# A hybrid trunk layer on one core: a list scheduler inside the kernel draws up every engine's order

## The chip, the core and the metric

The kernel runs on one core of a Trainium2 chip. The metric is device time in microseconds, the median of several runs. Three runs of the kernel before took 1523.97, 1532.54 and 1538.36 us, so the median is 1532.54 us.

## The reference

One residual layer over 16 learned meta tokens and 1024 tokens of width 1024, all float32:

- Input: RMS norm `hn` of the tokens, then one input projection `proj = hn @ w_in` to 7832 channels, split into three groups of heads.
- Gated DeltaNet, 6 heads of 128: causal convolution of four taps and SiLU on q, k, v; L2 norms of q and k; a gated delta rule over the tokens (`S_t = exp(g_t) (I - beta_t k_t k_t^T) S_{t-1} + beta_t k_t v_t^T`, `o_t = S_t^T q_t / sqrt(128)`); RMS norm and SiLU gate.
- RWKV-7, 8 heads of 64: token shift, low-rank decays and in-context rates, the recurrence `S_t = S_{t-1} diag(w_t) + (S_{t-1} a_t) b_t^T + v_t k_t^T`, group norm, a bonus term, SiLU gate.
- Mamba-2, 12 heads of 64 in 4 groups: convolution and SiLU, a chunked state-space scan, skip term, SiLU gate, grouped RMS norm.
- Output: `out = mixed @ w_out` (2048 to 1024), RMS norm, added to the input. The meta tokens are dropped.

## The kernel before, in words

Tokens lie along the free axis for the projections. The normalised input is kept in two float32r parts (`hh`, `hl`), each weight tile of 128 channels too, and a projection of one tile is three pieces of some 346 tokens, each of 8 x 3 matrix products that add up in one PSUM bank (`proj`, L154). In the profile these are the rows `pj`. The output projection works the same way on `ome`/`omw` and `ow` (rows `po`), with 512 columns a product.

The scans are cut into twelve units: six heads of DeltaNet (`unit_a`, a0 to a5), four pairs of heads of RWKV-7 (`unit_b`, b0 to b3) and two of Mamba-2 (`unit_c`, c0 and c1). Each unit first projects what its scan starts from ("proj"), then runs through small products in float32 with evacuations on ScalarE and VectorE between them ("scan"). Units a and b also solve triangular systems in blocks of 32 on VectorE (`solve32`, L189; rows `s_tmp`, `alb`, `blb`), after a trip through DRAM that regroups the blocks. Small products run on part of the array: 32 x 32 in the merges (`am`, `bm`), 64 rows or columns in `bsi`, `bu`, `bgr`. Values, queries and gates are projected later, when the scan needs them soon (`later`). Products of the units by name: `akT` starts the scan part of a unit a and `aoT` ends it; `bw` and `byT` do so for b, `cxT` and `cyT` for c. `unit_o` does the output projection in two halves: the first 512 columns with the channels that are finished, as a filler beside the last scans, and the rest when no other unit is active ("hold").

What sets the order: every unit is a generator that yields after a part. `schedule` (L1169 on) keeps a clock that adds up a rough length of what TensorE is given (`Meter`, L79), and an estimate of how long a scan part's results take to come back (`lag`). It emits the next scan part when its estimated time has come, and one product of a projection otherwise. Units start in the order of `PLAN`, when their tiles fit in the 26 slots of the pool. A unit's scan gets one of two lanes with two PSUM banks each; the lane with fewest units is taken, so units can share one. The framework then orders the emitted instructions on every engine by its own cost model and by priority: evacuations of projections are emitted with `high_priority(EVA)`, 700, scan parts with `PRI`, 300, and the solver's parts with `CALM`, 1500. It places all semaphores. SP issues the loads and stores.

Of the kernel before, what the change touches and what calls it, by code (L numbers as in the profile page):

```python
# [14 lines left out]
F32 = mybir.dt.float32  # L15
# [7 lines left out]
KT = 8  # L23
# [14 lines left out]
LOOK, LATE, EVAC, DMA = 0.05, 0.3, 2.0, 5.0  # L38
NOA = 3
PIPE = 0.5  # L40
HURRY, DUES = 60, (50, 60, 45, 55, 25, 60)
GATE = 9
XP = 500
# [6 lines left out]
SLOW = 1.0  # L50
# [28 lines left out]
class Meter:  # L79
    """An engine that adds up about how long what it is given takes: on the tensor engine, or on the way back to it."""  # L80

    def __init__(self, trunk, engine, fixed, each):
        self.trunk, self.engine, self.fixed, self.each = trunk, engine, fixed, each

    def __getattr__(self, name):
        op = getattr(self.engine, name)

        def call(out, *args, **kw):
            n = int(np.prod(out.shape[1:]))
            if name == "matmul":  # L90
                self.trunk.pe += n / 2400 if args[0].dtype == F32R else max(n, args[0].shape[-1]) / 600
            elif name == "transpose":
                self.trunk.pe += n / 1200
            elif not self.trunk.aside:
                self.trunk.lag += self.fixed + n * self.each
            return op(out, *args, **kw)  # L96

        return call


class Trunk:
    def __init__(self, tc, a):
        self.tc, self.nc, self.a = tc, tc.nc, a
        self.lane, self.pe, self.lag, self.aside = 0, 0.0, 0.0, False
        self.fetched, self.prefetch = {}, lambda i: None
        nc = tc.nc
        self.engines = tuple(Meter(self, e, f, n) for e, f, n in (
            (nc.vector, 0.25, 1 / 960), (nc.scalar, 0.3, 1 / 1200), (nc.tensor, 0, 0), (nc.gpsimd, 0.3, 1 / 500), (nc.sync, DMA, 0)))

    @contextmanager  # L110
    def off(self):
        """For instructions that nothing in their part waits for."""
        self.aside = True
        yield
        self.aside = False

# [11 lines left out]
    def tmp2(self, name):  # L128
        return self.sm.tile([128, 2, 128], F32, tag="t2", name=name, bufs=1)
# [12 lines left out]
    def weights(self, i):  # L142
        nc = self.nc
# [10 lines left out]
    def proj(self, i, pieces, evac, halo=0):  # L154
        """Channels of tile i, tokens along the free axis; a piece starts halo tokens early."""
        w = self.fetched.pop(i, None) or self.weights(i)
        for n, (a, b) in enumerate(pieces):
            a0 = max(a - halo, 0)
            p = self.pp.tile([128, 512], F32, tag="proj", name=f"pj{i}_{n}")
            for kt in range(KT):  # L160
                for m, (x, h) in enumerate(((0, self.hh), (0, self.hl), (1, self.hh))):
                    self.engines[2].matmul(p[:, : b - a0], w[kt // 4][:, x, kt % 4, :], h[:, kt, a0:b],
                                           start=(kt == 0 and m == 0), stop=(kt == KT - 1 and m == 2))
                    yield
            with self.tc.high_priority(EVA):
                evac(p, a, b, a - a0)
# [3 lines left out]
    def conv(self, i, cw, acc, bias=None, pieces=FULL):  # L170
        """Projection, causal convolution of four taps, halved (taps and bias hold halves), and silu(2x) = x tanh(x) + x."""
# [30 lines left out]
    def setup(self):  # L202
# [15 lines left out]
        pk = cp.tile([128, sum(n for _, n in PACK)], F32, tag="pack", name="pack")  # L218
# [23 lines left out]
        for cc in XG:  # L242
# [5 lines left out]
            with self.tc.high_priority(XP):  # L248
# [14 lines left out]
        # the gates are computed with tanh of the half; derived per-channel scalars of the RWKV group  # L263
# [7 lines left out]
    def scalars(self):  # L271
        """Per-token step sizes, decays and gates of the DeltaNet and Mamba groups."""
# [36 lines left out]
        # softplus(x) = max(x, 0) + log1p(u), u = exp(-|x|); log1p(u) = 2 atanh(u / (2 + u))  # L309
# [43 lines left out]
        # the same decays with tokens along the free axis, through DRAM, to be repeated over partitions  # L353
# [12 lines left out]
    def unit_a(self, h):  # L366
# [16 lines left out]
        # decays between the tokens of a chunk (rows the earlier one), masked before the exponential  # L383
# [12 lines left out]
        # |k|^2 and |q|^2 of each token  # L396
# [4 lines left out]
        for cc, p in transposed(k, "akT", groups):  # L401
# [6 lines left out]
            yield PIPE  # L408
        # the system is solved for the new values over bd = beta / |k|^2 and |k|
# [11 lines left out]
        # lo <- the strict part  # L421
        for gi, cc in enumerate(groups):
# [7 lines left out]
            yield PIPE  # L430

        # blocks of 32, solved with one block per partition
# [16 lines left out]
        yield 0.0  # L449
# [8 lines left out]
        # the values; up <- attention  # L458
        yield from self.wait(valued)
        vt = self.one([128, 9, 128], f"avt{h}")  # L460
        for cc, p in transposed(v_, "avT", groups):
# [3 lines left out]
            yield PIPE  # L465
        yield from self.wait(asked)
        for cc, p in transposed(q, "aqT", groups[:2]):
# [3 lines left out]
            yield PIPE  # L471
        v.tensor_scalar(ss[:, 9:], ss[:, 9:], EPS, None, ADD)
        self.rsqrt(rs[:, 9:], ss[:, 9:], "a_q")
        self.lag = 0.0
        for gi, cc in enumerate(groups[:2]):
# [6 lines left out]
            yield PIPE  # L482
        yield 7
        # dd: the blocks not transposed; merge 32 -> 64
# [10 lines left out]
        for i, (f, s) in enumerate(fs):  # L495
# [4 lines left out]
            yield 0.6  # L500
        for i, (f, s) in enumerate(fs):
# [4 lines left out]
            if i == 0:  # L506
                yield 0.6
# [4 lines left out]
                yield 0.3  # L512
        yield
        # merge 64 -> 128
# [20 lines left out]
        # the scan over chunks  # L535
        oss = sm.tile([128, 8], F32, tag="a_oss", name="a_oss", bufs=3)
        st = None
        for c in range(9):
# [22 lines left out]
            if c:  # L561
# [7 lines left out]
                self.lag = max(0.2, self.lag - 0.43)  # L569
# [3 lines left out]
        # rms norm of o (with q's norm and 1/sqrt(dk) folded in), gate  # L573
# [21 lines left out]
    def shifted(self, i, ti, t, gate=False):  # L595
        """Projection, mixed with the token before; PADB zero tokens in front. t: chunks of 64. gate: 2 silu of it."""
# [21 lines left out]
    def b_low(self):  # L618
        """The low-rank inputs of all heads, split in two, kept in DRAM."""
# [9 lines left out]
        # of both, the rounded part over its rest  # L629
# [8 lines left out]
    def unit_b(self, p):  # L638
# [11 lines left out]
        # each factor carries its decay to or from the chunk's end  # L650
# [12 lines left out]
        for i, (out, bias) in enumerate(((e1[:, :, 1:], self.w0), (at, self.a0))):  # L663
            for s, e in ((0, 8), (8, 16), (16, 17)):
# [4 lines left out]
                yield PIPE  # L669
# [499 lines left out]
    def schedule(self, plan, out, swap):  # L1169
# [29 lines left out]
        def step(s):  # L1199
            if s["want"] is not None:  # L1200
                s["has"], s["want"] = s["want"], None
# [173 lines left out]
```

## Time and profile before

| | |
|---|---|
| median of three runs | 1532.54 us |
| lowest and highest run | 1523.97 and 1538.36 us |
| span of the profiled execution, first to last instruction | 1518.0 us |
| mean granted TensorE clock | 0.970 |
| TensorE records (share of the span) | 1427.0 us (94%) |
| VectorE, ScalarE, GpSimd | 1014.6, 647.8, 239.2 us |
| instructions | 25,931, of which 9657 matrix products |

The profile is of one execution, and its span leaves out what lies before the first and after the last instruction; the views show no time for that. Matrix products are pipelined and their ends are modelled, so their records overlap: a covered TensorE is not one at its peak, and the pace is read from one start to the next. The granted clock (PEclk) is 1.00 at 2.4 GHz and 0.50 at 1.2 GHz. Names on the left of an arrow are written, those on the right read.

### The profile page before, as it was taken

The numbers are of one execution on the slowest core, as the hardware profiler recorded it, in microseconds if no ns is written. First come the engines' busy times: TensorE is split into PE (matmuls) and PEld (weight loads), VectorE is DVE, ScalarE is ACT, GpSimd is POOL, SyncE is SP. The second block draws the span as 40 slices with busy tenths as digits, with TensorE's granted clock in tenths as the row PEclk, the third lists the DMA queues.
The fourth block names the chain that finished last, engine by engine and source line by source line (L and its number), as shares of the span: only waits on it lengthen the run. The fifth ranks groups of instructions, "written<-read, shape, count | busy, mean of one in ns | idle before, by whom it ended". The sixth has DMA issues, their size and how long they took to land.

```text
span 1518.0 us, 25931 instructions
## 1 busy us (share of the span) xinstructions
PE 1427.0 (94%) x9657; PEld 1259.6 (83%) x9657; DVE 1014.6 (67%) x2688; ACT 647.8 (43%) x1814; POOL 239.2 (16%) x227
## 2 busy tenths in 40 slices
PE   4999999999999999997999999999999999889897
PEld 3988878887888888987888898899998988678686
DVE  7549695476659456869735699745489967542573
ACT  5354351334434352443635534433456154532530
POOL 2122011011101111223101221102232111200100
PEclk9999998899999999999989999989999999999999
DMA  5221211111011121211111111101322111552851
GB/s 187 58 85 43 70 33 39 29 41 64 29 30 47 49 74 43 86 31 53 46 43 50 43 46 53 36 29 57 97 59 61 43 36 44 169 159 89 250 193 56
DMA packets 102880, 104.28 MB, mean 69 GB/s; under 512 B 37915, under 2 KB 70427, under 8 KB 102755
## 3 DMA queue, kind: packets, MB, share of 16 engines
q1 hardware_dynamic: 102755, 102.64, 22.0%
q8 instruction: 76, 1.25, 0.3%
q14 instruction: 49, 0.40, 0.1%
HBM read 85.00 MB, written 17.60 MB: 68 GB/s over the span
## 4 chain that ended last, share of the span: by engine, by line
PE 30%; DVE 14%; issue 5%; ACT 4%; DMA 3%; POOL 0%; SPq 0%; DVEq 0%; ACTq 0%; POOLq 0%
PE pj L96 14%; PE po L96 5%; DVE s_tmp L96 3%; DVE alb L96 2%; PE am L96 2%; DMA or<-in_w_out_dram 2%; PE bsi L96 1%; DVE aq L181 1%; DMA omrw<-d_mix 1%; PE aops L96 1%; PE ads L96 1%; DVE av L181 1%; PE aks L96 1%; PE av L96 1%; ACT clt L904 1%
## 5 line engine op out<-in xcount | busy, mean ns | idle before, releaser
L96 PE MATMUL pj<-hh,w 128*128 128x350 f32 (+8 forms) x2928 | 773.9, 338 | 0.2 <-ACT hh L261 0.2
L96 PEld LDWEIGHTS pj<-hh,w 128*128 128x128 f32 x2928 | 516.7, 192 | 13.2 <-issue 2.1
L96 PE MATMUL pj<-hl,w 128*128 128x350 f32 (+8 forms) x1464 | 493.4, 337 | 0.0
L150 POOL TENSOR_TENSOR w<-wr,w 128x512 fp32r<-128x512 f32 x122 | 173.6, 1424 | 870.3 <-ACT w L149 631.7
L96 PEld LDWEIGHTS pj<-hl,w 128*128 128x128 f32 x1464 | 281.3, 192 | 6.6 <-issue 0.9
L149 ACT CAST w<-wr 128x512 fp32r<-128x512 f32 x122 | 74.9, 615 | 75.8 <-PE pj L96 64.4
L96 PE MATMUL po<-ow,omw 128*128 128x512 f32 x408 | 95.5, 395 | 6.2 <-ACT omw L1064 3.7
L96 PEld LDWEIGHTS po<-ow,omw 128*128 128x128 f32 x408 | 77.2, 190 | 24.6 <-ACT omw L1064 4.4
L96 PE MATMUL po<-ow,ome 128*128 128x512 f32 x360 | 90.6, 399 | 4.6 <-ACT ow L1046 1.8
L96 PEld LDWEIGHTS po<-ow,ome 128*128 128x128 f32 x360 | 66.6, 188 | 20.1 <-POOL ow L1047 2.5
L96 DVE TENSOR_TENSOR alb<-alb,s_tmp 33x30 f32<-33x30 f32 (+9 forms) x180 | 71.2, 395 | 1.0
L96 DVE TENSOR_TENSOR s_tmp<-alb 33x30 f32<-33x30 f32 (+9 forms) x180 | 67.4, 375 | 0.9
L96 DVE TENSOR_TENSOR buv<-bu,b_ib 64x128 f32<-64x128 f32 x68 | 19.1, 281 | 69.5 <-PE bu L96 69.3
L96 PE MATMUL bsi<-buv,bgm 64*64 64x64 f32 (+1 forms) x528 | 61.5, 238 | 0.0
L96 PEld LDWEIGHTS bsi<-buv,bgm 64*64 64x64 f32 (+1 forms) x528 | 42.1, 139 | 17.5 <-issue 2.2
L828 ACT COPY by<-bsi 64x128 f32<-64x128 f32 x64 | 16.7, 262 | 82.3 <-PE bsi L96 81.8
L181 DVE SCALAR_TENSOR_TENSOR cbc<-pj,pack,cbc 128x346 f32<-128x346 f32 (+4 forms) x72 | 40.5, 568 | 14.3 <-ACT cbc L178 13.5
L96 DVE SCALAR_TENSOR_TENSOR b_s<-bd,b_wc,b_s 64x64 f32<-64x64 f32 x120 | 34.0, 283 | 23.2 <-PE bd L96 18.2
L96 DVE TENSOR_TENSOR blb<-blb,s_tmp 68x30 f32<-68x30 f32 (+14 forms) x120 | 46.5, 387 | 1.1
L96 PE MATMUL bgr<-bar,bbk 64*128 64x128 f32 x272 | 43.8, 328 | 2.6 <-DVE bbk L96 2.0
L1065 DVE TENSOR_TENSOR ome<-omre,ome 128x512 fp32r<-128x512 f32 (+2 forms) x40 | 22.4, 594 | 34.1 <-ACT ome L1064 34.0
L1047 POOL TENSOR_TENSOR ow<-or,ow 128x512 fp32r<-128x512 f32 x16 | 21.0, 1316 | 135.9 <-ACT ow L1046 135.9
(324 smaller groups left out, 2414.7 us busy)
## 6 DMA issues: line engine op xcount, KB each, us to landing
wr<-in_wt_dram SPq DMA_DIRECT2D x122, 256.0 KB, 2.6
or<-in_w_out_dram SPq DMA_DIRECT2D x32, 256.0 KB, 2.6
omrw<-d_mix SPq DMA_DIRECT2D x32, 256.0 KB, 4.7
clt<-d_cs SPq DMA_DIRECT2D x24, 256.0 KB, 4.5
omre<-d_mix SPq DMA_DIRECT2D x24, 256.0 KB, 4.2
btw<-d_tw SPq DMA_DIRECT2D x8, 544.0 KB
x<-in_x_dram SPq DMA_DIRECT2D x8, 512.0 KB, 7.0
oxr<-in_x_dram SPq DMA_DIRECT2D x8, 512.0 KB
```

The source lines that it names most:

```text
L96: return op(out, *args, **kw)
L149: nc.scalar.copy(w[:, 0], raw)
L150: nc.gpsimd.tensor_tensor(w[:, 1], raw, w[:, 0].bitcast(F32), SUB)
L181: nc.vector.scalar_tensor_tensor(acc[:, a + z: b], p[:, o + z - s: o + b - a - s], cw[:, 3 - s: 4 - s], acc[:, a + z: b], MUL, ADD)
L828: nc.scalar.copy(yt[hs[(c - 1) % 2], (c - 1) // 2, :], pq[64:128, 0:128])
L904: nc.scalar.activation(t[:, e, i], t[:, e, i], AF.Exp, bias=self.ncs[:, 1 + 4 * w + i, k + e: k + e + 1])
L1047: (nc.vector if k % 2 else nc.gpsimd).tensor_tensor(t[:, 1], raw, t[:, 0].bitcast(F32), SUB)
L1065: nc.vector.tensor_tensor(t[:, 1], raw, t[:, 0].bitcast(F32), SUB)
```

## The change

Set-up and the low-rank projection (`setup`, `b_low`) are emitted as before. From there on nothing is emitted at once: `Scribe` stands in for each engine and writes down every instruction with its engine, the earlier instructions that it depends on (worked out from the memory it reads and writes, and from the earlier users of its buffer), a modelled step, a modelled delay until its result is seen, and a class: `pj` products of projections, `scan`, `ev` evacuations of projections, `ld` weight loads, `calm` the solver, `off` what nothing in its part waits for. Each unit, each late projection, the weight loads and `scalars` are tasks, with one queue per engine in program order. The scheduler takes again and again the instruction with the earliest modelled start over all engines and emits it; a link without semaphore to the one emitted before it on that engine fixes the order. The framework still places the semaphores.

TensorE chooses between the first projection product and the first scan product that are ready: in bursts of at least 1.0 us of projections, then a round of scan products; a running average of the array's work (over 3 us) below 0.36 puts projections first. The other engines take, among what could start within 0.05 us of the earliest, the one with the smallest ready time plus a handicap by class. Lags, priorities and fractions at the yields are gone. A lane is given to one unit only. The plan has a new order. The slots of a unit are counted free only when its instructions are emitted. What is computed stays the same.

```diff
-LOOK, LATE, EVAC, DMA = 0.05, 0.3, 2.0, 5.0
-PRI, EVA, CALM = 300, 700, 1500
+BURST, JOIN = 1.0, 0.25
+COOL, COLD = 3.0, 0.36
+LESS = {"scan": 0.0, "ev": 0.3, "ld": 0.5, "calm": 1.0, "off": 0.4}
+AHEAD = 8
-PLAN = "a0 b0 b1 b2 c0 b3 a1 a2 a3 c1 a4 a5"
+PLAN = "a0 b0 b1 a1 c0 b2 a2 c1 b3 a3 a4 a5"
...
+SEES = {"PE": 0.055, "ACT": 0.035, "DVE": 0.035, "POOL": 0.075, "SP": 0.027}
...
+        if key == "PE":
+            rows, cols = args[0].shape[0], int(np.prod(args[0].shape[1:]))
+            fast = name == "matmul" and args[0].dtype == F32R
+            i.mode = (r(rows), r(cols), fast)
+            i.step = (n / 2400 + 0.013 if fast else 0.109 if name == "transpose" else
+                      0.063 if r(cols) == 32 else 2 * max(0.058 if r(cols) == 64 else 0.112, n * 0.00085))
+            i.work = rows * cols / 16384 * n * (1 if fast or name == "transpose" else 2) / 2400
+            i.extra = {128: 0.165, 64: 0.108, 32: 0.07}[r(cols)]
+        elif key == "DVE":
+            i.step = 0.065 + n * (0.00116 if len(ins) > 2 else 0.00105)
+        elif key == "ACT":
+            i.step = 0.105 + 0.00078 * n if name == "copy" else 0.14 + 0.00086 * n
+        elif key == "POOL":
+            i.step = 0.04 + n * (0.0024 if name == "tensor_tensor" else 0.001)
+        else:
+            last = min(a.ap[-1][1] if a.ap[-1][0] == 1 else 1 for a in (out, args[0]))
+            total = int(np.prod(out.shape)) * 4
+            i.step, i.extra = 0.46, total / 380e3 * (1 if last >= 128 else 1.5 if last >= 32 else 4)
...
+    def emit(self, i, start):
+        r = i.go()
+        ins, was = r.ins, self.before.get(i.eng)
+        if was is None:
+            self.tc.keep_in_program_order(r)
+        else:
+            self.tc.add_manual_dep(ins, was, mybir.DependencyInfo(mybir.DependencyClass.NoSync, mybir.DependencyReason.DATA), reason="order")
+        self.before[i.eng] = ins.name
+        if i.eng == "PE":
+            if self.array and self.array != i.mode:
+                if self.array[:2] != i.mode[:2]:
+                    start += 0.093
+                if i.mode[2] and not self.array[2]:
+                    i.step += 0.1
+            self.array = i.mode
+        self.free[i.eng] = start + i.step
+        if i.eng == "SP":
+            self.bus = max(self.bus, start + 0.4) + i.extra
+            i.done = max(start + 2.0, self.bus + 1.3)
+        else:
+            i.done = start + i.step + i.extra
...
-            with self.tc.high_priority(EVA):
+            with self.of(cls="ev"):
                 evac(p, a, b, a - a0)
...
+                for s in list(active):
+                    if s["kind"] != "scan" or s["drop"] and s["want"] is None or s["task"].q["PE"] or s["task"].n > AHEAD:
+                        continue
+                    if s["on"] and not s["on"]["done"] or not safe(s):
+                        continue
+                    if s["lane"] is None:
+                        open_ = [g for g in range(len(GB)) if all(o["lane"] != g for o in active)]
+                        if not open_:
+                            continue
+                        s["lane"] = open_[0]
...
+                if e == "PE":
+                    now = self.free["PE"]
+                    pj = min((h for h in heads if h[2].cls == "pj"), key=lambda h: h[0], default=None)
+                    sc = [h for h in heads if h[2].cls != "pj"]
+                    sc = min(sc, key=lambda h: (h[0] > now + 0.02 if h[2].out == last else 1, h[0]), default=None)
+                    if pj is None or sc is None:
+                        pick = sc or pj
+                    elif heat * float(np.exp((self.seen_at - now) / COOL)) < COLD:
+                        pick = pj
+                    elif round_:
+                        pick = sc if sc[0] <= max(now + JOIN, pj[0]) else pj
+                    else:
+                        pick = sc if since >= BURST and sc[0] <= max(now + 0.03, pj[0]) or sc[0] < pj[0] - 0.3 else pj
+                else:
+                    first = min(h[0] for h in heads)
+                    pick = min((h for h in heads if h[0] <= first + 0.05), key=lambda h: h[1] + LESS[h[2].cls])
+                if best is None or pick[0] < best[0]:
+                    best = pick
```

## Rows read from the trace of the kernel before

**Rows 1.** The page's heading and its part 1, busy time by engine.

```profile
span 1518.0 us, 25931 instructions
PE 1427.0 (94%) x9657; PEld 1259.6 (83%) x9657; DVE 1014.6 (67%) x2688; ACT 647.8 (43%) x1814; POOL 239.2 (16%) x227
```

**Rows 2.** Chain that ended last: start us, length us, what, how many; two undisturbed stretches.

```profile
1057.40 11.51 PE pj L96 x72
...
1441.05 68.99 PE po L96 x303
```

**Rows 3.** Groups by line (columns as in part 5 of the page): the projections' products.

```profile
L96 PE MATMUL pj<-hh,w 128*128 128x350 f32 (+8 forms) x2928 | 773.9, 338 | 0.2 <-ACT hh L261 0.2
...
L96 PE MATMUL pj<-hl,w 128*128 128x350 f32 (+8 forms) x1464 | 493.4, 337 | 0.0
...
L96 PE MATMUL po<-ow,omw 128*128 128x512 f32 x408 | 95.5, 395 | 6.2 <-ACT omw L1064 3.7 <-DVE ob L1141 2.5
L96 PE MATMUL po<-ow,ome 128*128 128x512 f32 x360 | 90.6, 399 | 4.6 <-ACT ow L1046 1.8 <-POOL ow L1047 1.5 <-ACT ome L1064 1.2
```

**Rows 4.** Busy time by stretches of 100 us: length, engines, PEclk, DMA share, GB/s.

```profile
0.00:100.00 100.00, 78.45 (x477) 73.13 (x478) 57.16 (x155) 48.03 (x117) 24.11 (x33) 0.98 0.35 120
...
700.00:800.00 100.00, 87.26 (x693) 75.66 (x692) 63.61 (x207) 42.70 (x134) 16.21 (x10) 0.88 0.15 45
...
1000.00:1100.00 100.00, 98.92 (x643) 95.06 (x641) 54.41 (x115) 42.94 (x102) 21.93 (x17) 1.00 0.22 69
```

**Rows 5.** Timeline from 708: start us, length us, engine, what [idle before <-releaser].

```profile
720.71 0.66 PE L96 MATMUL avT<-pack,av 128*128 128x128 f32 x2 [9.60 <-DVE av L184]
```

**Rows 6.** Busy time by stretches: before the longest low-clock piece, in it, all ten pieces.

```profile
238.00:252.00 14.00, 13.00 (x150) 10.70 (x150) 9.52 (x15) 2.70 (x7) 1.41 (x3) 0.99 0.14 39
...
251.90:279.20 27.30, 27.30 (x139) 21.15 (x139) 9.49 (x19) 3.74 (x10) 0.00 (x0) 0.50 0.04 7
...
sum 88.60, PE 83.99 PEld 70.42 DVE 41.49 ACT 19.70 POOL 1.82; mean PE 8.40 PEld 7.04 DVE 4.15 ACT 1.97 POOL 0.18
```

**Rows 7.** Timeline of TensorE: first and last return to a projection, one change at 464.

```profile
24.27 0.63 PE L96 MATMUL pj<-hh,w 128*128 128x336 f32 x1
...
464.02 0.32 PE L96 MATMUL pj<-hh,w 128*128 128x336 f32 x1
464.33 0.45 PE L96 MATMUL bsi<-buv,bgm 128*64 128x64 f32 x4
464.71 0.42 PE L96 MATMUL pj<-hh,w 128*128 128x336 f32 x1
464.96 0.32 PE L96 MATMUL pj<-hl,w 128*128 128x336 f32 x1
...
1343.39 1.86 PE L96 MATMUL po<-ow,ome 128*128 128x512 f32 x7
```

**Rows 8.** Timeline of TensorE at 248: two scans' products in turn.

```profile
248.63 0.48 PE L96 MATMUL bgr<-bar,bbk 64*128 64x128 f32 x2
249.05 0.24 PE L96 MATMUL bm<-bdd,bgm 32*32 32x32 f32 x2
249.22 0.48 PE L96 MATMUL bgr<-bar,bbk 64*128 64x128 f32 x2
```

**Rows 9.** By tile: duration ns min/median/max, first and last start us, forms.

```profile
L96 PE MATMUL akT<-pack,ak x54: 270/272/329, 78.7 to 1145.1; 128*128 128x128 f32 x48, 128*16 128x128 f32 x6
...
L96 PE MATMUL aoT<-pack,avt x48: 270/273/328, 229.4 to 1343.4; 128*128 128x128 f32 x48
...
L96 PE MATMUL bw<-btw,bw x48: 192/395/628, 98.9 to 637.0; 128*128 128x512 f32 x32, 128*128 128x64 f32 x16
...
L96 PE MATMUL byT<-pack,by x32: 272/273/328, 362.4 to 913.9; 128*128 128x128 f32 x32
...
L96 PE MATMUL cxT<-pack,cx x54: 270/273/330, 485.7 to 1092.1; 128*128 128x128 f32 x48, 128*16 128x128 f32 x6
...
L96 PE MATMUL cyT<-pack,cx x48: 271/273/332, 741.3 to 1312.5; 128*128 128x128 f32 x48
```

More of the change, by code (lines that the diff above doesn't have):

```diff
@@ L9 @@
+from collections import defaultdict
 from contextlib import ExitStack, contextmanager
@@ L76, in nt, with __init__ @@
     return NM if c == 0 else 128
-class Meter:
-    def __init__(self, trunk, engine, fixed, each):
-        self.trunk, self.engine, self.fixed, self.each = trunk, engine, fixed, each
+class Instr:
+    __slots__ = ("go", "eng", "deps", "cls", "step", "extra", "mode", "work", "start", "done", "task", "out")
+class Task:
+    def __init__(self, name):
+        self.name, self.q = name, {e: [] for e in ENGINES}
+        self.n = 0
+ENGINES = ("PE", "ACT", "DVE", "POOL", "SP")
+SEES = {"PE": 0.055, "ACT": 0.035, "DVE": 0.035, "POOL": 0.075, "SP": 0.027}
@@ L85, in __getattr__, with __init__ @@
+class Scribe:
+    def __init__(self, trunk, key, engine):
+        self.trunk, self.key, self.engine = trunk, key, engine
     def __getattr__(self, name):
-        op = getattr(self.engine, name)
+        op, t = getattr(self.engine, name), self.trunk
+        if not t.writing:
+            return op
         def call(out, *args, **kw):
[L89 to L96, printed above, removed]
@@ L98, in __getattr__, with __init__, tile @@
-        return call
+            t.write(self.key, name, op, out, args, kw)
+        return call
+class Engines:
+    def __init__(self, trunk, nc):
+        self.vector, self.scalar, self.tensor = (Scribe(trunk, k, e) for k, e in (("DVE", nc.vector), ("ACT", nc.scalar), ("PE", nc.tensor)))
+        self.gpsimd, self.sync = Scribe(trunk, "POOL", nc.gpsimd), Scribe(trunk, "SP", nc.sync)
+class Pool:
+    def __init__(self, trunk, pool, bufs):
+        self.trunk, self.pool, self.bufs, self.made = trunk, pool, bufs, defaultdict(list)
+    def tile(self, shape, dt, tag, name, bufs=None):
+        t = self.pool.tile(shape, dt, tag=tag, name=name, **({} if bufs is None else {"bufs": bufs}))
+        if self.trunk.writing and tag != "s":
+            made, n = self.made[tag], bufs or self.bufs
+            key = t.tensor.name
+            if len(made) >= n:
+                old = made[-n]
+                self.trunk.born[key] = [a[2] for a in self.trunk.seen.get(old, ())]
+            made.append(key)
+        return t
@@ new lines, in ready @@
+    def ready(self, i):
+        if i.start is None:
+            t = 0.0
+            for d in i.deps:
+                if d.done is None:
+                    return None
+                if not d.eng == i.eng == "PE":
+                    t = max(t, d.done + SEES[i.eng])
+            i.start = t
+        return i.start
+    def emit(self, i, start):
[19 more added lines that the diff above has]
+            i.done = start + i.step + i.extra
+        i.start, i.go = start, None
+        i.deps = ()
+        i.task.q[i.eng].pop(0)
+        i.task.n -= 1
@@ L128, in tmp2 @@
     def tmp2(self, name):
-        return self.sm.tile([128, 2, 128], F32, tag="t2", name=name, bufs=1)
+        return self.sm.tile([128, 2, 128], F32, tag="tw", name=name, bufs=1)
     def rsqrt(self, y, x, tag, pool=None):
@@ L1159, in later @@
     def later(self, i, gen, due):
-        self.queue.append({"tile": i, "gen": gen, "due": self.clock + due, "done": False, "t": 0.0})
+        self.queue.append({"tile": i, "gen": gen, "due": self.free["PE"] + due, "done": False})
         self.gates -= 1
@@ L1167, in wait, with begin_writing @@
             yield gate
+    def begin_writing(self):
+        self.writing, self.tasks, self.loader = True, [], Task("loader")
+        self.tasks.append(self.loader)
+        self.fixed = {t.tensor.name for t in (self.hh, self.hl, self.pk0, self.mu1, self.ka1, self.d0)}
     def schedule(self, plan, out, swap):
-        units, active, self.queue, self.fetched, self.clock = plan.split(), [], [], {}, 0.0
+        units, active, self.queue, self.fetched = plan.split(), [], [], {}
         self.gates = sum({"a": 3, "b": 2, "c": 3}[u[0]] for u in units)
@@ new lines, in schedule @@
+        while True:
+            advance()
+            best = None
+            for e in ENGINES:
+                heads = []
+                for t in self.tasks:
+                    if t.q[e]:
+                        i = t.q[e][0]
+                        r = self.ready(i)
+                        if r is not None:
+                            heads.append((max(r, self.free[e]), r, i))
+                if not heads:
+                    continue
+                if e == "PE":
[11 more added lines that the diff above has]
+                        pick = sc if since >= BURST and sc[0] <= max(now + 0.03, pj[0]) or sc[0] < pj[0] - 0.3 else pj
+                else:
+                    first = min(h[0] for h in heads)
+                    pick = min((h for h in heads if h[0] <= first + 0.05), key=lambda h: h[1] + LESS[h[2].cls])
+                if best is None or pick[0] < best[0]:
+                    best = pick
+            if best is None:
+                left = [t.name for t in self.tasks if t.n]
+                if left or units or active or self.queue or fill or out:
+                    raise ValueError(f"no part fits: {left} {units} {[(s['name'], s['has'], s['want'], s['drop'], s['kind']) for s in active]}")
+                break
+            start, _, i = best
+            if i.eng == "PE":
+                was = self.free["PE"]
+                if i.cls == "pj":
+                    since = since + i.step if not round_ else i.step
+                    round_ = False
+                else:
+                    round_ = True
+                last = i.out
+                heat = heat * float(np.exp((self.seen_at - start) / COOL)) + i.work / COOL
+                self.seen_at = start
+            self.emit(i, start)
+            self.tasks = [t for t in self.tasks if t.n or t is self.loader or any(t is s["task"] for s in active) or fill and (
+                t is fill.get("task") or fill.get("unit") and t is fill["unit"]["task"]) or planned and planned.get("unit") and t is planned["unit"]["task"]]
```

284 lines of the change are left out of this document (182 added, 102 removed).

## The prediction

> **What bounds the kernel now.** I read the page's heading first, then the engines by 100 us, then TensorE's own rows. TensorE bounds the kernel: its records cover 1427.0 of 1518.0 us [rows 1]. That says little about its pace, because records overlap; the floor has to come from starts. A projection product runs at 11.51 / 72 = 0.160 us when nothing disturbs it, an output product at 68.99 / 303 = 0.228 us [rows 2]. There are 2928 + 1464 = 4392 of the first and 408 + 360 = 768 of the second [rows 3], so undisturbed they take 703 + 175 = 878 us. The other 640 us of the span hold the products of the scans and four kinds of loss:
>
> - *Idle*: 1518.0 - 1427.0 = 91 us. The first 100 us hold 21.5 of it, the stretch from 700 holds 12.7, the one from 1000 only 1.1 [rows 4]. The longest wait is typical: a transpose of the values (avT) sat 9.60 us at the head of TensorE's order, though projections stood behind it because VectorE had not yet done the last step of their convolution (av, L184) [rows 5].
> - *Low clock*: in 88.6 us, in ten pieces, the granted clock is 0.50, the lower level of 1.2 GHz; there TensorE's records cover 84.0 us [rows 6]. Work there takes about double, so about half, 88.6 / 2 = 44 us, is lost.
> - *Changes between projections and scans*: I counted 572 stretches of scan products with a projection behind them in TensorE's timeline; rows 7 hold the first and the last such projection and one whole change. From the projection of 464.02 to the one of 464.96 is 0.94 us: two projections at 0.160, four 64-column products, and both changes. The four follow one another within 0.45 us with the pipelined end of the last; I put their own share at a rough 0.24, which leaves 0.94 - 0.32 - 0.24 = 0.38 us for the changes. A stretch of full 128 x 128 products changes no tile shape, and I put it at 0.02 us at least. Half way, 0.2 x 572 = 114 us.
> - *Changes between two scans*: at 248.63 two Gram products are followed by two 32 x 32 products and the next pair comes 0.59 us later [rows 8]; half of that, 0.3, I estimate as the changes. This term lies partly within the 114 us.
>
> **The change part by part.**
> *Recording and fixed orders.* The engines' instructions stay the same in kind and number (25,931 [rows 1]); the recorder runs while the program is built. The links between neighbours on an engine carry no semaphore. I cost this at nothing. What is new is that every engine, SP and POOL too, must keep exactly the order which the kernel's own model drew up. Where the model is off, the head of a queue waits and all behind it wait. The nearest row for that is the 9.60 us wait [rows 5], since the order of before was fixed in advance as well. Bounds: 0 and some 10 such waits, +96 us. I take 0 net, as the idle term below is already cut short for it.
>
> *VectorE, ScalarE, POOL and SP pick what is ready first, with a handicap by class* (scan 0, evacuation 0.3, load 0.5, solver 1.0 us). In before the solver had priority 1500 and evacuations 700, so solver steps went ahead of the convolution, which is what stands behind the wait in rows 5. With the new handicaps the convolution goes first. Such waits end; what is late next is the solver, off TensorE's path unless lanes run out (rival below). Of the 91 us idle the first 21.5 stay, since set-up keeps its old order. Of the other 69.5 us I take 33 as saved; bounds 0 and 60.
>
> *TensorE in rounds.* A projection burst now lasts at least 1.0 us, some six or seven products at 0.160 us, unless none can run or a scan would be 0.3 us earlier; then both lanes' ready products go together, a bank's group kept together by the "last" rule. Of the 114 us a quarter goes, 28: some 95 fewer stretches at 0.2 us are 19, and 30 alternations like that of rows 8 at 0.3 us are 9. Bounds: -45, and +20 if the scans need a round of their own for each step (100 more stretches).
>
> *Projections preferred while little of the array has worked.* Before the longest low piece, 251.9 to 279.2, the engine was covered for 13.00 of 14 us, but by 150 small products; within it 139 [rows 6]. Putting projections among these raises the share of the array at work. Of the 44 us I take 33 as saved. Each insertion costs about 0.3 us (the 0.38 of rows 7 for a wider product, less a little); three for each of ten units with 32-wide products is 9 us. Net -24; bounds -40 and +9.
>
> Here a rule of the Trainium skill speaks against the change: by "TensorEngine Tiling (Array Packing)", Key Properties, changing the tiling mode, not just the tile, drains the engine. The trace agrees, with 0.31 us from the start of the last projection to the first narrow product, where the next projection would have come after 0.160 [rows 7]. By the rule alone the preference only adds drains, +9 instead of -24.
>
> *Lanes and plan.* A lane of two banks now belongs to one unit until its end; before, a third unit could share one. The plan puts a1 before c0 and c1 before b3, which mixes long and short units. I take 0 here; bounds 0 and the rival's price.
>
> *Sum.* -33 (idle) - 28 (changes) - 24 (clock) = -85 us on the profiled execution's span: 1518.0 to 1433. The median of the three runs is 1532.5, that is 14.5 us above the span; the views don't show how much of that lies around this execution. Adding it gives **1447.5 us**, 5.5% faster.
>
> **The rivals.**
> *The two lanes become the bound (slower).* Units a run from akT to aoT, the first from 78.7, the last to 1343.4; units b from bw to byT, from 98.9 to 913.9; units c from cxT to cyT, from 485.7 to 1312.5 [rows 9]. Taking for each of the twelve its own first and last start in these views, I get 1052 us for six a, 1089 for four b, 538 for two c: 2679 us. In two lanes that is 1340, from 79 to 1419, where before the last scan ended at 1343. Behind it stand 408 output products, 93 us, and about 19 for stores, loads and the end: 1531 of span, 1545 measured with even lanes; a third of a unit uneven (60 us), half of it covered, makes **1575**. It decides where the units' times add up to over 2 x (1343 - 79) = 2528 us, so where they shrink by less than 6%. For it: before had three in flight around 1137 to 1260, and the solver now yields. Against it: the shortest of each kind (152, 245, 255) add up to 2402, and a scan's steps now come at most about 1.5 us apart, near the pace of before.
> *The order is as good as before, no better (no change).* The new model errs in other places, waits return elsewhere, and the low clock falls elsewhere: 1517 to 1548. For it: TensorE is already covered for 94%. Against it: [rows 5] and [rows 8] are losses that the new picks name directly.
> *Nearly all goes (much faster).* The upper ends together, -60 - 45 - 40 = -145, give 1373 of span, **1387.5**. For it: 1000 to 1100 shows that TensorE can run so [rows 4]; against it: that stretch is nearly all projections.
> *The clock falls as before.* If a low clock came from idle gaps alone, inserting projections would win nothing: 1447.5 + 24 = 1471.5. For it: one low piece stands behind the 9.60 us wait. Against it: the longest has 1.0 us of idle in the 14 us before it [rows 6].
> The Trainium skill, "TensorE: Matmul & The Clock Gate", section on HAM oscillation, puts the practical rule as avoiding idle gaps between bursts. The trace does not bear it out as the whole cause, as rows 6 show.
>
> **How the numbers follow.** Forecast 0.50 (own range 1405 to 1500); clock unaided 0.10; nearly all 0.12; no change 0.11; lanes 0.17. A measurement here tells about 1% from no change, that is 1517 to 1548. Faster 0.50 + 0.10 + 0.12 = 0.72, same 0.11, slower 0.17. The range goes from 1385, the upper ends together, to 1550, which takes in no change and the lanes' case when they are even; about 0.16 stays above and 0.03 below.
>
> **What would show it.** Right: idle of TensorE outside the first 100 us falls to about 36; the 0.50 pieces add up to some 30 us; fewer than 500 changes back to projections, hardly any projection burst under 1 us; no wait over 5 us by a transpose for a convolution. Wrong: TensorE idle in whole stretches before the output's second half while both lanes wait on VectorE or DMA (lanes); units' times above 2528 us in all; or new waits of several us at the head of ScalarE or VectorE for a DMA that the model had earlier.

## The result and the profile after

The changed kernel takes **1645.93 us** (median of 1640.47 to 1647.01), against 1532.54 before: a ratio of 1.0746, 95% interval 1.0684 to 1.0808. It is 7.5% slower where I forecast 5.5% faster, and it lies far above my range.

The heading and part 1 of the page, to be laid beside [rows 1]:

```profile
span 1645.3 us, 25976 instructions
...
PE 1470.0 (89%) x9657; PEld 1311.0 (80%) x9657; DVE 1027.6 (62%) x2688; ACT 649.4 (39%) x1814; POOL 230.4 (14%) x227
```

The span grew by 127.3 us. TensorE's records grew by 43.0 us, so its idle time grew by 84.3: from 91.0 to 175.3 us. The same 9657 products were also done at a lower clock; mean 0.931 after 0.970. Busy time by stretches, against [rows 4]:

```profile
0.00:100.00 100.00, 73.94 (x414) 67.98 (x414) 51.16 (x134) 41.78 (x93) 18.98 (x27) 0.93 0.33 110
700.00:800.00 100.00, 93.21 (x689) 81.31 (x689) 70.61 (x213) 50.68 (x156) 13.79 (x14) 0.97 0.18 57
1000.00:1100.00 100.00, 90.83 (x551) 85.91 (x551) 66.73 (x151) 31.50 (x91) 14.83 (x13) 0.88 0.13 33
1200.00:1300.00 100.00, 79.58 (x517) 72.08 (x516) 67.46 (x207) 40.47 (x140) 17.17 (x17) 0.87 0.14 43
1400.00:1500.00 100.00, 88.73 (x376) 72.35 (x377) 31.64 (x71) 31.11 (x71) 7.70 (x6) 0.90 0.40 120
```

The stretch from 700, which had 12.7 us of idle, has 6.8; the one from 1000, which had 1.1, has 9.2. From 1200 to 1300 a fifth of the time is empty although projections are left to do. So the loss isn't one hole, it is spread. What TensorE waits for (line, awaited instruction, us in total, times, longest), beside the 9.60 us of [rows 5]:

```profile
PE czT L207 <- DVE ctmp L207: 15.8, 6, 4.9
...
PE akT L207 <- ACT akT L207: 10.5, 5, 5.5
PE po L207 <- ACT ow L207: 9.5, 1, 9.5
PE ads L207 <- ACT a_vn L207: 8.3, 6, 5.2
PE am L207 <- DVE add L207: 8.0, 3, 5.0
PE agk L207 <- DVE alo L207: 7.8, 3, 4.7
```

The long wait of avT for a convolution is gone. In its place stand many waits, most of them of up to 5.5 us for answers of VectorE and ScalarE to the scans; the one of 9.5 us is for weights of the output projection. Behind the first 100 us, 78 us of TensorE's waits now end with VectorE and 63 with ScalarE; before it was 46 and 13. The longest of the first line shows how one comes about. TensorE's timeline:

```profile
688.94 0.32 PE L207 MATMUL pj<-hl,w 128*128 128x336 f32 x1
694.17 0.90 PE L207 MATMUL czT<-pack,cz 128*128 128x128 f32 x3 [4.91 <-DVE ctmp L207]
```

ScalarE and VectorE in that time; of VectorE's solver steps the last three of a row are shown:

```profile
687.74 0.50 ACT L207 ACTIVATE ctmp<-czT 128x384 f32<-128x384 f32 x1
...
692.38 0.40 DVE L207 TENSOR_TENSOR blb<-blb,s_tmp 68x240 f32<-68x240 f32 x1
692.81 0.40 DVE L207 TENSOR_TENSOR s_tmp<-blb 68x238 f32<-68x238 f32 x1
693.25 0.40 DVE L207 TENSOR_TENSOR blb<-blb,s_tmp 68x238 f32<-68x238 f32 x1
693.58 0.54 DVE L207 SCALAR_TENSOR_TENSOR ctmp<-ctmp,czT 128x384 f32<-128x384 f32 x1
```

ScalarE had done its part at 688.24. VectorE's part of 0.54 us stood behind solver steps in the fixed order until 693.58, and the next transpose, which needs the PSUM bank that this part reads, stood at the head of TensorE's order with projections behind it. Solver steps in front are not the whole of it: of the 140 us that TensorE waited between its products behind the first 100 us, VectorE spent 27 on solver steps. Three stretches around this wait (columns as in [rows 4]):

```profile
686.00:689.20 3.20, 3.20 (x23) 2.96 (x21) 2.94 (x8) 0.84 (x2) 0.00 (x0) 1.00 0.00 0
689.20:693.20 4.00, 0.06 (x1) 0.00 (x0) 3.69 (x10) 0.00 (x0) 0.00 (x0) 1.00 0.00 0
693.20:700.00 6.80, 5.83 (x23) 5.77 (x24) 6.58 (x13) 3.38 (x12) 3.27 (x2) 0.50 0.00 0
```

The granted clock goes from 1.00 to 0.50 before the wait ends, and the 5.83 us of products behind it run at the lower level: a projection product starts every 0.28 us there, every 0.16 us before the wait. That is a second part of the price of such a wait. All 26 such pieces together, beside the ten of [rows 6]:

```profile
sum 225.20, PE 196.08 PEld 171.38 DVE 125.23 ACT 64.47 POOL 32.03; mean PE 7.54 PEld 6.59 DVE 4.82 ACT 2.48 POOL 1.23
```

In 24 of the 26 I found at least 1.1 us of waiting of TensorE in the 7 us ahead of the piece, a length that I chose for counting; in all stretches of that length from 100 us on it is 22 in 100. In the kernel before it was so for 3 of the ten pieces only, so the clock falls without such a wait too. Half of what is covered there is 196.08 / 2 = 98 us lost, before 83.99 / 2 = 42: 56 more. Idle and clock make 84 + 56 = 140 us of the 127; the stretches of scan products, counted as before, fell from 572 to 396, which at my 0.2 us is 35 gained. This account, with half of the covered time as an estimate of the loss, closes to some 20 us, no better.

The lanes: first and last products of the units, against [rows 9].

```profile
L207 PE MATMUL akT<-pack,ak x54: 270/272/383, 85.8 to 1284.4; 128*128 128x128 f32 x48, 128*16 128x128 f32 x6
L207 PE MATMUL aoT<-pack,avt x48: 270/272/328, 278.5 to 1427.1; 128*128 128x128 f32 x48
```

Each unit taken by its own first and last start, six a come to 995 us, four b to 1004, two c to 362: 2361 us, less than the 2679 of before and less than the 2528 from which the lanes would decide. The last scan still ends 84 us later, at 1427.1. The other 43 us of the longer span lie behind it, in the output projection: 218.2 us follow there after 174.7, with 36.2 us of idle TensorE after 15.5, 30.5 us at the lower clock after 6.6, and 745 output products still to do after 685.

### The profile page after: what moved, and what is told of

Read it like the earlier page. It is cut to its first block, busy times and chain, and to the rows that moved or that the text cites. A ratio compares the mean times of both kernels' runs of the same rounds, so it can differ in the third digit from the quotient of the medians.

```text
span 1645.3 us, 25976 instructions
## 1 busy us (share of the span) xinstructions
PE 1470.0 (89%) x9657; PEld 1311.0 (80%) x9657; DVE 1027.6 (62%) x2688; ACT 649.4 (39%) x1814; POOL 230.4 (14%) x227
## 4 chain that ended last, share of the span: by engine, by line
PE 43%; DVE 28%; DMA 9%; ACT 8%; issue 8%; SPq 2%; POOL 1%; DVEq 0%; ACTq 0%; POOLq 0%
PE pj L207 20%; PE po L207 6%; DVE s_tmp L207 4%; PE bgr L207 2%; DVE alb L207 2%; PE bsi L207 2%; DMA omrw<-d_mix 2%; DMA wr<-in_wt_dram 2%; DVE blb L207 2%; PE am L207 2%; DMA blb<-d_l 1%; DVE cx L207 1%; DVE clt L207 1%; SPq L207 1%; DMA or<-in_w_out_dram 1%
## 5 line engine op out<-in xcount | busy, mean ns | idle before, releaser
L207 PE MATMUL pj<-hh,w 128*128 128x350 f32 (+8 forms) x2880 | 762.2, 341 | 2.7 <-POOL w L207 1.5
L207 PEld LDWEIGHTS pj<-hh,w 128*128 128x128 f32 x2880 | 523.8, 198 | 15.9 <-issue 3.9
L207 POOL TENSOR_TENSOR w<-wr,w 128x512 fp32r<-128x512 f32 x120 | 163.9, 1386 | 961.3 <-ACT w L207 852.6
L207 PE MATMUL po<-ow,omw 128*128 128x512 f32 x408 | 104.7, 417 | 27.0 <-ACT po L207 10.6
L207 PEld LDWEIGHTS po<-ow,omw 128*128 128x128 f32 x408 | 81.5, 202 | 50.3 <-ACT po L207 13.5
L207 PE MATMUL po<-ow,ome 128*128 128x512 f32 x360 | 84.9, 396 | 4.4 <-ACT ome L207 4.4
L207 ACT CAST w<-wr 128x512 fp32r<-128x512 f32 x120 | 69.5, 616 | 36.2 <-DMA wr<-in_wt_dram 35.8
L207 DVE TENSOR_TENSOR alb<-alb,s_tmp 33x30 f32<-33x30 f32 (+9 forms) x180 | 66.2, 368 | 3.3
L207 DVE TENSOR_TENSOR s_tmp<-blb 68x30 f32<-68x30 f32 (+14 forms) x120 | 46.1, 384 | 22.4 <-DMA blb<-d_l 20.2
L207 DVE TENSOR_TENSOR omw<-omrw,omw 128x512 fp32r<-128x512 f32 x32 | 21.9, 692 | 47.3 <-ACT omw L207 46.7
```

What stands on the lines that cost most here:

```text
L207: i.go, i.eng, i.cls, i.task, i.done, i.start = (lambda: op(out, *args, **kw)), key, self.cls, self.task, None, None
```

## The experiments

All leave the computation as it is. Each was timed beside the kernel before on the same chip, whose medians there were 1528.5 to 1538.0.

**Lanes and plan, alone in the kernel before.** The first gives a lane to one unit only, the second also takes the new plan.

```diff
+            open_ = [g for g in range(len(GB)) if all(o["lane"] != g for o in active)]
...
-                    s["lane"] = used.index(min(used))
+                    s["lane"] = open_[0]
```

```diff
-PLAN = "a0 b0 b1 b2 c0 b3 a1 a2 a3 c1 a4 a5"
+PLAN = "a0 b0 b1 a1 c0 b2 a2 c1 b3 a3 a4 a5"
```

> The kernel before, with its own scheduler, order and plan; only a lane is given to one unit until its end, as after. Theory A (two exclusive lanes are the bound, as the lanes' rival had it): the last scan ends near 1420 instead of 1343 us and the time rises to 1580 to 1650. Theory B (an order fixed on a model that is too quick): lanes cost little here, 1530 to 1560.

> As e1, and with the plan of the kernel after. Theory A: as e1 or worse, 1580 to 1650, if the plan leaves a lane empty while the seven tiles of a unit c are projected. Theory B: within 2% of before, since the plan only changes which units meet.

Measured: 1505.11 us, ratio 0.9845 (0.9789 to 0.9901), and 1516.31, ratio 0.9883 (0.9846 to 0.9919). Lanes of their own don't cost anything, they gain 1.5%, which is more than both theories expected, and the plan costs some 11 us of it, with intervals that overlap. The lanes' rival falls.

**The links and the preference, taken from the changed kernel.**

```diff
         else:
-            self.tc.add_manual_dep(ins, was, mybir.DependencyInfo(mybir.DependencyClass.NoSync, mybir.DependencyReason.DATA), reason="order")
+            pass
```

```diff
-                    elif heat * float(np.exp((self.seen_at - now) / COOL)) < COLD:
+                    elif False:
```

> The kernel after without the links that hold each engine to the emitted order; the framework may reorder by its own model. Theory B: waits at the head of TensorE (175 us idle after) fall back towards 91, the 0.50 pieces shrink from 227 us towards 100, time 1540 to 1580. Theory A: the lanes still hold, 1620 to 1660.

> The kernel after without the preference for projections while little of the array was at work; all else as after. If the preference delays the scans' chains: 1600 or less. If it works as meant (my forecast gave it 24 us): 1660 to 1680. Theories A and B both expect little, 1630 to 1660.

Measured: 1513.21 us without links, below what either theory expected, ratio 0.9898 (0.9722 to 1.0074), and 1650.61 without the preference, ratio 1.0797 (1.0712 to 1.0881). Heading and part 1 without links:

```profile
span 1522.5 us, 25926 instructions
...
PE 1444.1 (95%) x9657; PEld 1290.4 (85%) x9657; DVE 1005.7 (66%) x2688; ACT 640.5 (42%) x1814; POOL 239.4 (16%) x227
```

The recording, the plan, the lanes and all the picks are still there; only the line that ties each instruction to its neighbour is gone, and the framework orders each engine again. Idle time falls from 175.3 to 78.4 us and the time by 133. So the links make the whole loss. The low clock doesn't go back all the way: in this execution, the slower of the two, sixteen pieces cover more than the ten of before.

```profile
sum 163.80, PE 154.99 PEld 133.16 DVE 76.96 ACT 56.31 POOL 29.08; mean PE 9.69 PEld 8.32 DVE 4.81 ACT 3.52 POOL 1.82
```

The preference is worth 5 us here, within the scatter.

**On which engine.** One condition in `emit` keeps the links on some engines; the engine was TensorE, all but TensorE, VectorE, ScalarE, and GpSimd with SP.

```diff
-        else:
+        elif i.eng == "PE":
```

> As the kernel after, with order links on TensorE alone; the other engines are ordered by the framework. Theory P (TensorE's own fixed order makes the waits): near after, 1620 to 1650. Theory V (the other engines' fixed orders hold back the results that TensorE waits for): near e3, 1510 to 1550.

> As the kernel after, with links on VectorE, ScalarE, GpSimd and SP, none on TensorE. Theory P: near e3, 1510 to 1550. Theory V: near after, 1600 to 1650. If both have a share, the two excesses over e3 add up to about 130 us.

> As the kernel after, with links on VectorE alone. Theory V with the solver's steps on VectorE as its core: 1570 to 1640. Otherwise near e3, 1510 to 1540.

> Links on ScalarE alone. VectorE alone cost 1581.7 - 1513.2 = 68 us, TensorE alone 46, all but TensorE 154. If the loss is in every engine that answers TensorE's scans, ScalarE alone costs 30 to 80 us: 1545 to 1595. If VectorE's solver is what stands in front, ScalarE alone costs nothing: 1500 to 1530.

> Links on GpSimd and the transfers' queue alone. If the loss is in the loads (a transfer put behind one that waits 41 us for GpSimd), this costs 40 us or more: over 1550. If the loss is in the order of the engines that answer TensorE, it costs nothing: 1500 to 1530.

| links on | us | more than without links |
|---|---|---|
| TensorE | 1559.48 | 46 |
| VectorE | 1581.71 | 68 |
| ScalarE | 1559.15 | 46 |
| GpSimd and SP | 1583.49 | 70 |
| all but TensorE | 1667.36 | 154 |
| all | 1645.93 | 133 |

No engine is free of it and the shares don't add up (46 + 68 + 46 + 70 = 230). VectorE alone and the loads alone came out as the expectations had it that put the loss in the solver's steps and in the loads, ScalarE as the one that put it in every engine that answers; TensorE alone and all but TensorE missed both their ranges. But no engine is the one place, since each of the four runs with a part of the links costs 46 us or more, and all but TensorE cost no less than all.

With the links on TensorE alone 99.7% of its products stand at the same place as in the changed kernel, and still the time is 86 us shorter: the new order of TensorE by itself makes 46 us, and the rest needs the orders of the other engines, where VectorE's instructions differ by 4 places and ScalarE's by 2 in the middle. (1513.21 is the middle of two runs at 1502.18 and 1524.25, so each difference is good to some 10 us.)

How the loads come to cost 70 is only in part visible. With links on GpSimd and SP alone TensorE waited 18.3 us for weights (`w`), without links 2.7. In the changed kernel SP, where a transfer whose turn has not come holds all behind it, waited 41.1 us at once for a solver's tile; without links the longest such wait for `alb` is 33.6 us, so these rows don't settle it:

```profile
SPq L207 <- DVE alo L207: 132.1, 6, 25.5
SPq L207 <- DVE alb L207: 122.2, 4, 41.1
```

**Is it the charges of the kernel's model?** All links stay. One run lets transfers land later in the model; another also charges TensorE 1.08 times and VectorE 0.4 us for each weight subtraction on GpSimd; a third lets results be seen 0.3 to 0.4 us later.

```diff
-            i.done = max(start + 2.0, self.bus + 1.3)
+            i.done = max(start + 2.0, self.bus + 1.3) + i.late
```

```diff
+        if i.eng == "PE":
+            i.step *= 1.08
+        if i.eng == "POOL" and i.cls == "ld":
+            self.free["DVE"] = max(self.free["DVE"], start) + 0.4
```

```diff
-SEES = {"PE": 0.055, "ACT": 0.035, "DVE": 0.035, "POOL": 0.075, "SP": 0.027}
+SEES = {"PE": 0.4, "ACT": 0.3, "DVE": 0.3, "POOL": 0.4, "SP": 0.3}
```

> All links as after, but the model's transfers land later by what the traces show: 3.2 us for the regrouped blocks read back, 2.6 for the decays repeated over partitions, 1.3 for the mixed channels, 0.4 for inputs. Theory T (the model's transfers are too quick, and the order built on them makes the waits): 1580 or less, with idle of TensorE below 140 us. If the error lies elsewhere, above all in the low clock that the model does not know: 1620 to 1650.

> All links stay; the transfers land later in the model as in the run before with later transfers, TensorE's steps are charged 1.08 times, and each weight subtraction on GpSimd charges VectorE 0.4 us (139 of them, 56 us in all, against 52 us that VectorE's instructions ran over their usual time beside GpSimd in the changed kernel's trace). Theory of wrong charges: the fixed orders lose 133 us because the model is too quick, so most of it comes back: 1560 us or less. Theory of rigid orders: no model is close enough over 26,000 instructions, so hardly anything comes back: 1610 to 1660.

> All links stay; the model sees a result of another instruction 0.3 to 0.4 us after its end instead of 0.03 to 0.08, so it puts other work between an instruction and the one that needs it. Rigid orders without reserve: with a reserve of 0.3 us a small delay is no longer handed on, so a third or more of the 133 us comes back: 1600 or less. Wrong charges of single operations: the waits are of 2 to 5 us, far over 0.3, and stay: 1620 to 1680.

Measured: 1644.89, 1646.72 and 1640.14 us. None is told from 1645.93. Better charges, as far as I could read them from the trace, and a reserve of 0.3 us bring nothing back, and the reserve refutes my theory of orders without reserve in the form that I gave it.

**How far apart are the instructions that want to change places?** The link goes to the instruction 8, or 64, places ahead instead of to the neighbour.

```diff
-        ins, was = r.ins, self.before.get(i.eng)
+        ins, line = r.ins, self.before.setdefault(i.eng, [])
...
-        else:
-            self.tc.add_manual_dep(ins, was, ...
+        elif len(line) >= 64:
+            self.tc.add_manual_dep(ins, line[-64], ...
```

> On every engine an instruction is linked to the one eight places ahead of it instead of to its neighbour, so the framework may exchange neighbours within eight places. If the loss is made of near exchanges (two or three instructions in the wrong turn), half of the 133 us or more comes back: 1580 or less. If it is made of far ones (25 solver steps ahead of one product of the gate, a memset ahead of weights for tens of us), little comes back: 1610 to 1660.

> The same with 64 places. If the far exchanges make the loss, this is near the kernel without links, 1513: 1500 to 1560, while eight places stay above 1600. If neither number helps, it is not the place in the order but something that the links do in themselves, such as added waits: 1600 or more.

Measured: 1597.66 us (ratio 1.0437, 1.0360 to 1.0514) with 8 places, between the two theories, and **1501.88** (ratio 0.9812, 0.9741 to 0.9882) with 64. With 64 places nearly as many links stand as before, so it isn't the links in themselves. Eight places give back 48 us, 64 the whole. Heading and part 1 with 64 places:

```profile
span 1498.0 us, 25920 instructions
...
PE 1411.8 (94%) x9657; PEld 1268.2 (85%) x9657; DVE 1008.9 (67%) x2688; ACT 642.1 (43%) x1814; POOL 245.0 (16%) x227
```

Its twelve pieces at the lower clock together, from the busy time by stretches:

```profile
sum 95.60, PE 86.85 PEld 77.72 DVE 52.87 ACT 26.82 POOL 12.97; mean PE 7.24 PEld 6.48 DVE 4.41 ACT 2.24 POOL 1.08
```

Idle is 86.2 us and the low clock covers 86.9, both near the 91.0 and 84.0 of before. TensorE's order moved by few places from the changed kernel's, but it is another: it has 532 stretches of scan products where the changed kernel has 396. I matched the two traces, the first of each kind with the first and so on, and half of TensorE's products stand in the same place, three quarters within 12 places. On average projections stand 8 places earlier, the c units' `cof` 40 and `cds` 30 later. On VectorE half stand within 2 places; the DeltaNet solver's steps come 11 later on average, convolutions of values 12 earlier.

**Whose place is it?** The obvious reading was the solver, so its class was left out of the links, then the weights' loads, casts and subtractions too.

```diff
-        if was is None:
+        if i.cls in ("calm",):
+            pass
+        elif was is None:
...
-        self.before[i.eng] = ins.name
+        if i.cls not in ("calm",):
+            self.before[i.eng] = ins.name
```

> All links, but the instructions of the solver's class stay out of them (600 of VectorE, 72 transfers and 10 of GpSimd): they may stand anywhere, all others keep the model's order. In the run with 64 places the solver's steps on VectorE came 11 places later and the convolutions 12 earlier. If the solver's place is the main loss, two thirds of 133 - 90 us or so - come back: 1530 to 1570. If it is the order in general, in which the solver has a share like its share of the instructions, 20 to 40 us come back: 1600 to 1630.

> The same, and the weights' loads, casts and subtractions are free too (120 each on the transfers' queue, ScalarE and GpSimd). In the run with 64 places the casts came 12 places earlier on ScalarE. If loads that are put behind waiting work are a part of the loss, 20 us or more under the run with the solver free; if not, within 10 us of it.

Measured: 1650.65, outside both ranges, and 1650.32 us: nothing. But the free solver hardly moved. VectorE's instructions moved by 1 place or less in three quarters of all cases, though by up to 17, and the DeltaNet solver's steps came 1 place later on average (3.5 with the loads free too), where it is 11 with 64 places and 22 without links. So these runs don't test the solver's place; they show that freeing it is no help while the rest of the order stands. The weights' casts did move, 15 places earlier on ScalarE where it is 13 with 64 places, and nothing came of it: their place alone isn't the cause. **Open** is which exchanges make up the loss, among the solver, scans, evacuations and projections.

**The preference without links, and the quickest version again.** The two edits are those above.

> No links and no preference for projections. My forecast's term for the preference was 24 us, so 1513 + 24 = 1537. With the links it was worth 5 us, within the scatter: if that holds here, 1505 to 1525, and the clock's mean stays near the 0.945 of the run without links.

> The kernel before with lanes of their own, the quickest so far at 1505.1. If that is a gain of its own and not chance, it comes again at 1500 to 1512, 1.2 to 2.0% under the kernel before of the same chip.

Measured: 1506.02 us (0.9834, 0.9777 to 0.9891) and 1503.95 (0.9823, 0.9766 to 0.9880). Without links too the preference gains nothing: 1506.0 without it, 1513.2 with it. The gain of lanes of their own came again, on another chip. Three versions thus beat the kernel before by 1.7 to 1.9%, and the changed one by more, and can't be told from one another: lanes of their own in the kernel before, links 64 places back, and neither links nor preference. The first needs a few lines.

## Why the prediction was wrong

- **The step that failed is "Recording and fixed orders": "I take 0 net, as the idle term below is already cut short for it".** The links cost 133 us, more than my upper bound of 96. I had said that the order of before was fixed in advance as well, and took one 9.60 us wait of it [rows 5] for the nearest row. That comparison was the error. Without links the order is fixed in advance too, by the framework, and the time is 133 us shorter; a different order drawn up from the same recording is what costs. The row told how long one wait is, and nothing of how many there would be. And I bounded idle time alone, not the clock that falls with many of the waits.
- *Idle.* Forecast 91 less 33; it became 175.3. Outside the first 100 us it is 175.3 - 26.1 = 149 us against the 36 that I named as the sign of being right. Without links it is 78.4, a gain of 12.6. The wait that I named did go, as said; a total of others took its place. In the one shown above solver steps still stand ahead of a step that a scan needs, which the handicaps by class were to prevent.
- *Changes.* The direction was right, the count above mine: 176 fewer stretches instead of 95, and bursts of projections under 1 us fell from 359 to 5. But this holds only where the links hold TensorE's order: without them there are 556 stretches, with 64 places 532, and these are the quicker kernels. So longer rounds go with the slower ones. Held on TensorE alone, the order with 396 stretches takes 46 us more than no links; whether the rounds themselves make that loss wasn't tried.
- *Clock.* Forecast 44 us of loss less 24; the pieces grew from 88.6 to 225.2 us. The links are not all of that: without them it was 163.8 us, with 64 places 95.6, in one execution each. The preference gained nothing in either of two comparisons. My rival on idle gaps was nearer the matter than I allowed, though its price (+24) was far too small, since it left the waits where they were. The Trainium skill's rule that I had called not borne out as the whole cause ("TensorE: Matmul & The Clock Gate", section on HAM oscillation: avoid idle gaps between bursts) agrees with 24 of 26 pieces here. But so much waiting stood ahead of only 3 of the ten pieces before and 8 of the sixteen without links, so idle gaps are not the whole cause, as I had said.
- *Lanes and plan.* Taken at 0. In the kernel before, lanes of their own gain 27 us; the plan gives some 11 of it back.
- *The rivals.* The lanes decide from 2528 us of units' times; 2361 were found, so this rival is refuted, and it stood for the wrong reason even though it was the slower side. "No change" and "nearly all" fell with the result. The sign that came true is the last I named, new waits of several us, but at the head of TensorE for VectorE and ScalarE, not for a DMA that the model had earlier; later landings in the model changed nothing.
- *The 14.5 us between span and median.* Most of it is scatter between executions: in the changed kernel's profiled run time and span lie 1.7 us apart (1647.01 and 1645.3). I carried it over unchanged from the median of before, so it moves no difference between the kernels.

## What to carry to other kernels

Fixing every engine's order from one's own model is an edit with a cost of its own: leave slack in the order (here links 64 places back, not to the neighbour) or leave the order to the framework, and price the recorder and the links apart. A wait of TensorE costs its length and, where the clock falls in it, about half of the products that follow at the lower level; bound both. When a large edit bundles five ideas, look for the one that was worth it by itself: here one unit to a lane, 1.5 to 1.8%.

## What the runs showed of the hardware

Short instructions on VectorE can be held while GpSimd subtracts on two inputs. VectorE, then GpSimd, in the changed kernel; the same form in other places takes 0.16 us:

```profile
196.22 1.24 DVE L207 SCALAR_TENSOR_TENSOR a_q_t<-a_q_t,a_rs 128x8 f32<-128x8 f32 x1
...
197.69 1.22 DVE L207 SCALAR_TENSOR_TENSOR a_rs<-a_q_t,a_rs 128x8 f32<-128x8 f32 x1
...
199.56 0.16 DVE L207 SCALAR_TENSOR_TENSOR a_q_t<-a_q_t,a_rs 128x8 f32<-128x8 f32 x1
...
196.02 2.87 POOL L207 TENSOR_TENSOR w<-wr,w 128x512 fp32r<-128x512 f32 x2 [12.06 <-ACT w L207]
```

In the changed kernel 69 instructions of VectorE ran over 0.3 us beyond the median of the same operation, tiles and shape, 59 us in all, and 66 of them overlapped such a subtraction of GpSimd; in the kernel before it was 83, 70 us and 75. So it explains no part of the difference. The Trainium skill states it ("GPSIMD Engine Reference", Specifications: its SBUF interfaces are shared with VectorE, with contention where a VectorE instruction has two SBUF inputs or is in a 2-port mode). The trace agrees for 60 of the 66, which are operations on two tensors; the other six are TENSOR_SCALAR, three of them on one tile, and the trace doesn't show their mode.
